# Joining the small steps of two slots in the RWKV time mixing

## The chip, the cores and the metric

The kernel runs on one NeuronCore of a Trainium2 chip. The metric is the device time of one execution in microseconds; lower is better. The program has no loops on the chip: Python writes out some 58,000 instructions, and a framework puts in the semaphores and orders the instructions of each engine when the program is built. TensorE (PE) multiplies matrices into PSUM, VectorE (DVE), ScalarE (ACT) and GpSimd (POOL) work elementwise, SyncE (SP) issues most DMAs.

## The reference

A trunk of two layers on 256 tokens of width 2048, batch 1, all float32. Layer 0 is RWKV-7 time mixing with 32 heads of 64, layer 1 attention in a band; each is followed by a squared-ReLU MLP. The change lies in the time mixing. There, with `r`, `k`, `v`, the decay `w` and the rates `a` and `g` projected from the normalised input:

```python
kk = heads(k * k_k)
kk = kk / jnp.maximum(jnp.sqrt(jnp.sum(kk * kk, axis=-1, keepdims=True)), 1e-12)
k = k * (1 + (a - 1) * k_a)
decay = jnp.exp(-jnp.exp(heads(w_log)))

def step(S, inp):
    r_t, w_t, k_t, v_t, kk_t, a_t = inp
    sa = jnp.einsum('bhvk,bhk->bhv', S, -kk_t)
    S = (S * w_t[:, :, None, :] + sa[..., None] * (kk_t * a_t)[:, :, None, :]
         + v_t[..., None] * k_t[:, :, None, :])
    y = jnp.einsum('bhvk,bhk->bhv', S, r_t)
    return S, y
```

The scan runs over the 256 tokens. Its output `y` is normalised by head, gets a bonus term `sum(r * k * r_k) * v`, is multiplied by `g` and projected by `w_o`.

## The kernel before

**Large products.** A projection weight comes from HBM in halves of 128x1024 float32 (`raw`, six buffers). `halves` (L371) turns each into two tiles: `wH` is a rounded copy made by ACT (L378), `wL` the rest, made by DVE (L381); each has three buffers (`W_BUFS`). `proj2` (L406) multiplies one k tile by two matmuls: `wH` with both parts of the activations (L412, 512 columns), `wL` with the first part (L413, 256 columns). A half weight holds eight k tiles.

**The chunked scan.** The 2048 channels are 16 pairs of heads (128 partitions each); a `Pair` object carries one pair through the time mixing in 36 steps. The 256 tokens are four chunks of 64. `early` (8 steps) makes the operands: decays (`cum`, `e0`, `e1`, `e2`), the normalised key `kk`, and `kr`, `bh`, `kh`, `vp`. `invert` (12 steps) forms for all chunks the products of `bh` with `kr` and inverts the unit triangular 64x64 matrices by levels: in each level, `tiles` (L107) multiplies 32x32 blocks twice, first with the transposed inverse so far (`tt`), then, after ACT has copied that product to `xs` (L243, at the last level L248), with `xs`. `late` (16 steps) goes through the four chunks in turn, three steps each (`g`; `sa`; the output `py` and the state `zs`), then normalises and gates. `head_sums` (L115) sums over each head by one matmul with a block matrix of ones; `each` (L105) is eight 64-row matmuls.

**The slots.** `layer_a` (L634) issues the work by slots (loop at L889). A pair starts every `SLOTS` = 8 slots, so four or five pairs are under way at once, each in another phase. In every slot each live pair takes one step, those in `invert` first, then `late`, then `early`. Behind them come two large steps (four k tiles) of the `k` and `r` projections of a coming pair (`proj_steps`), or, in the last 36 slots, steps of the output projection (`out_steps`). In three slots of four `self.ada()` adds a step of the adaLN vector, a product that DVE accumulates (L454). PE is held to this order by hand: each step's matmuls are tied behind the last PE instruction of the one before:

```python
for _, _, pr in sorted(live, key=lambda x: x[:2]):
    with tc.issue_after(last):
        next(pr.gen)
    last = self.last_pe()
```

The other engines' instructions are ordered by the framework when the program is built, by its own estimate of when each is ready. PSUM is shared out in tags: `ms` (`psm`, two buffers), `pj` (two), `gr` and `iv` (one each), `lt` (two, a bank per pair in `late`).

Of the kernel before, what the change touches and what calls it, by code (L numbers as in the profile page):

```python
# [24 lines left out]
NPAIR = D // P  # L25
# [52 lines left out]
class Pair:  # L78
# [13 lines left out]
    def s(self, name="s", bufs=8):  # L92
        return self.b.pw.tile([P, T], F32, tag=name, bufs=bufs, name=name)
# [28 lines left out]
    def early(self):  # L122
        b, nc, j, k, r, v, s, ch = self.b, self.b.nc, self.j, self.k, self.r, self.v, self.s, self.ch
        pw, vec, cst, e01 = b.pw, b.vec, b.cst, self.e01
        lw = self.lw
        z = b.psm()
        nc.tensor.matmul(z[:, 0:T], lw[:, 0, :], self.tw, start=True, stop=True)
        nc.tensor.matmul(z[:, T:2 * T], lw[:, 1, :], self.ta, start=True, stop=True)
# [12 lines left out]
        yield  # L141
        pss = b.psm()[:, :T]
        self.head_sums(pss, sq)
        cum = s()
        nc.vector.tensor_tensor_scan(out=cum, data0=cst("reset"), data1=sw, initial=0.0, op0=ALU.mult, op1=ALU.add)
        e0, e1 = e01[:, :, 0:C], e01[:, :, 1:C + 1]
        nc.scalar.activation(e1, ch(cum), AF.Exp, scale=-1.0)
        e2 = s()
        nc.scalar.activation(e2, cum, AF.Exp)
        self.pc = pw.tile([P, 4, 1], F32, tag="pc", bufs=4, name="pc")  # L150
        nc.gpsimd.tensor_copy(self.pc, e01[:, :, C:C + 1])
        yield
        rs, ss, rr = s(), s(), s()
        nc.vector.tensor_scalar(out=ss, in0=pss, scalar1=1e-24, scalar2=None, op0=ALU.max)
        nc.scalar.activation(rs, ss, AF.Ln)
        nc.scalar.activation(rs, rs, AF.Exp, scale=-0.5)
        nc.scalar.activation(rr, rs, AF.Square)
        km = s()
        nc.gpsimd.tensor_scalar(out=km, in0=a, scalar1=-1.0, scalar2=vec("k_a", j), op0=ALU.add, op1=ALU.mult)
        self.bh, self.kh = s("bh", 2), s("kh", 2)  # L160
        nc.gpsimd.tensor_tensor(out=self.bh, in0=a, in1=e2, op=ALU.mult)
        yield
        nc.vector.scalar_tensor_tensor(out=rr, in0=rr, scalar=-0.5, in1=ss, op0=ALU.mult, op1=ALU.mult)
        nc.vector.scalar_tensor_tensor(out=rs, in0=rr, scalar=1.5, in1=rs, op0=ALU.add, op1=ALU.mult)
        kk = s()
        nc.vector.scalar_tensor_tensor(out=kk, in0=k, scalar=vec("k_k", j), in1=rs, op0=ALU.mult, op1=ALU.mult)
        nc.vector.scalar_tensor_tensor(out=km, in0=km, scalar=1.0, in1=k, op0=ALU.add, op1=ALU.mult)
        yield
        kr = self.kr = self.big("kr", 4)
        nc.vector.tensor_tensor(out=kr[:, :, 0:C], in0=ch(kk), in1=e0, op=ALU.mult)  # L170
        nc.vector.tensor_tensor(out=self.bh, in0=self.bh, in1=kk, op=ALU.mult)
        nc.vector.tensor_tensor(out=kr[:, :, C:P], in0=ch(r), in1=e1, op=ALU.mult)
        rkp = s()
        nc.vector.scalar_tensor_tensor(out=rkp, in0=r, scalar=vec("r_k", j), in1=km, op0=ALU.mult, op1=ALU.mult)
        nc.vector.tensor_tensor(out=self.kh, in0=km, in1=e2, op=ALU.mult)
        yield

        self.vp = pw.tile([P, 4, C], F32, tag="vp", bufs=4, name="vp")
        pt = b.psm().rearrange("p (a c k) -> p a c k", a=2, c=4)
        self.each(lambda c: pt[:, 0, c, :], lambda c: ch(v)[:, c, :], lambda c: cst("cen"))  # L180
        nc.scalar.copy(self.vp, pt[:, 0])
        yield
        pbn = b.psm()[:, :T]
        self.head_sums(pbn, rkp)
        nc.vector.tensor_tensor(out=v, in0=pbn, in1=v, op=ALU.mult)
        yield
# [5 lines left out]
    def invert(self):  # L192
# [8 lines left out]


        ui = cst("ui").unsqueeze(1).to_broadcast([P, 4, P])
        ts = []
        for src in (bh, kh):
            t = s()
            nc.gpsimd.tensor_tensor(out=ch(t), in0=ch(src), in1=self.pc.to_broadcast([P, 4, C]), op=ALU.mult)
            ts.append(t)
        pg = pp.tile([P, 4, P], F32, tag="gr", bufs=1, name="gr")
        self.each(lambda c: pg[:, c, :], lambda c: ch(bh)[:, c, :], lambda c: kr[:, c, :])  # L210
        ar = self.ar = s("ar", 3)
        nc.vector.tensor_tensor(out=ch(ar), in0=pg[:, :, C:P], in1=ui[:, :, C:P], op=ALU.mult)


        da, co, u = half("da", 2), half("co", 2), half("u", 2)
        for i, K in enumerate(QS):
            n = H * (i % 2)
            nc.scalar.copy(da[K], pg[K, :, n:n + H])
            if i % 2 == 0:
                nc.scalar.mul(co[K], pg[K, :, H:C], -1.0)  # L220
        nc.gpsimd.tensor_tensor(out=u, in0=da, in1=every("lev0"), op=ALU.mult)
        als = b.pw.tile([P, 4, 4, H], F32, tag="al", bufs=2, name="al")
        nc.gpsimd.tensor_tensor(out=als, in0=da.unsqueeze(1).to_broadcast([P, 4, 4, H]),
                                in1=cst("levs").rearrange("p (l k) -> p l k", l=4).unsqueeze(2).to_broadcast([P, 4, 4, H]),
                                op=ALU.mult)
        yield
        nc.vector.tensor_tensor(out=u, in0=u, in1=every("eye_h"), op=ALU.add)

        pt = b.psm().rearrange("p (a c k) -> p a c k", a=2, c=4)
        for i, t in enumerate(ts):  # L230
# [4 lines left out]
        uf = self.u = b.uf[self.j % 2]  # L235
        down, up = ((0, 1), (2, 3)), ((1, 0), (3, 2))
        for l in range(1, 6):
            tt_, xs = half("tt", 2), half("xs", 2)
            nc.vector.transpose(out=tt_.rearrange("p c t -> p (c t)"), in_=u.rearrange("p c t -> p (c t)"))
            pi = self.corner(l)  # L240
            if l < 5:
                self.tiles(pi, als[:, l - 1], tt_, [(i, i) for i in range(4)])
# [9 lines left out]
            if l < 5:  # L252
                self.tiles(pi, xs, u, [(i, i) for i in range(4)])
                nc.vector.tensor_tensor(out=u, in0=u, in1=pi, op=ALU.add)
            else:
                self.tiles(pi, xs, u, up)
                for K in QS[::2]:
                    nc.vector.tensor_copy(uf[K, :, H:C], pi[K])
# [7 lines left out]
    def late(self):  # L266
# [7 lines left out]
        for c in range(4):  # L274
# [22 lines left out]
            if c < 3:  # L297
# [8 lines left out]
                else:  # L306
                    nc.vector.scalar_tensor_tensor(out=zn, in0=zs, scalar=pc[:, c, :], in1=pch[:, 2, :],
                                                   op0=ALU.mult, op1=ALU.add)
                zs = zn
            yield  # L310

        sq = self.square(py)
        yield
        var = b.psm()[:, :T]
        self.head_sums(var, sq)
        yield
        rg = s("sl", 1)
        nc.scalar.activation(rg, var, AF.Ln, scale=1.0 / C, bias=b.col(C_GN))
        nc.scalar.activation(rg, rg, AF.Exp, scale=-0.5)
        nc.vector.scalar_tensor_tensor(out=rg, in0=py, scalar=b.vec("ln_w", j), in1=rg, op0=ALU.mult, op1=ALU.mult)  # L320
        yield
        pg = b.psm()[:, :T]
        for i in range(2):
            mm(pg, lg[:, i, :], self.tg[:, i, :], start=(i == 0), stop=(i == 1))  # L324
# [5 lines left out]
class Body:  # L330
# [303 lines left out]
    def layer_a(self, st, sp):  # L634
# [198 lines left out]
        with ExitStack() as s1:  # L833
# [55 lines left out]
            for slot in range(S * NPAIR + Pair.STEPS):  # L889
# [342 lines left out]
```

## Time and profile before

| | |
|---|---|
| time, median of 3 runs | 2665.69 us (2665.36 to 2669.86) |
| profiled execution, its own time | 2668.82 us |
| its span, first to last instruction | 2667.0 us |
| mean granted clock of TensorE | 0.992 |
| time mixing by slots | about 203 to 711 us of the span |
| PE, DVE, ACT busy in 490 to 560 us | 69.29, 62.84, 40.58 us of 70 |

The profile is one execution with all engines' instructions. "Busy" is the time in which an engine had an instruction under way; matmuls are pipelined and their ends are modelled, so for PE the starts are what can be trusted. In a timeline a row gives the start, the duration, the engine, the source line, the operation, output and inputs by tile name, shapes and the count of merged instructions; square brackets give idle time ahead of it and what ended it. A float32 product appears as two matmul records. L12 is line 12 of the kernel.

### The profile page before, as it was taken

What the parts mean: (1) busy time and instruction counts of PE and PEld (TensorE: products, weight loads), DVE (VectorE), ACT (ScalarE), POOL (GpSimd) and SP (SyncE); (2) the same over time, 40 slices, a digit from 0 to 9 for tenths busy, and PEclk for the clock granted to TensorE, in tenths of its full rate; (3) what the DMA queues carried; (4) which work ended last, traced back from release to release, by engine and by line L of the source; (5) the groups of instructions that cost most, each with busy time, mean ns of one, the idle gap of its engine ahead of it and who ended that gap; (6) DMA issues with size and microseconds to landing.
All of it is one profiled execution on the core that took longest, in us unless ns stands there. A gap on an engine that the chain in (4) does not pass through costs nothing.

```text
span 2667.0 us, 58173 instructions
## 1 busy us (share of the span) xinstructions
PE 2594.2 (97%) x23596; PEld 2229.2 (84%) x23596; DVE 2112.8 (79%) x3102; ACT 1345.2 (50%) x2435; POOL 208.7 (8%) x320
## 2 busy tenths in 40 slices
PE   7999999999999999999999999999999999999997
PEld 4787777887899888888888998877898888888886
DVE  6788888889789888888888898899887555555555
ACT  3346455555456445355365554565564463453554
POOL 0002223322110000000001100000100000000002
PEclk9999999999999999999999999999999999999998
DMA  9976556566778888889898679887766555555553
GB/s 349 312 244 211 185 179 207 180 214 199 246 236 312 309 317 327 319 324 332 318 329 293 238 242 331 318 274 256 265 218 235 190 189 184 188 189 186 186 189 119
DMA packets 207149, 662.62 MB, mean 248 GB/s; under 512 B 21408, under 2 KB 54560, under 8 KB 206880
## 3 DMA queue, kind: packets, MB, share of 16 engines
q1 hardware_dynamic: 204816, 656.36, 71.5%
q8 instruction: 185, 3.03, 0.5%
q10 hardware_dynamic: 2064, 2.54, 0.3%
q14 instruction: 84, 0.69, 0.1%
HBM read 656.72 MB, written 2.10 MB: 247 GB/s over the span
## 4 chain that ended last, share of the span: by engine, by line
PE 85%; DVE 5%; issue 4%; DMA 4%; ACT 2%; POOL 1%; DVEq 0%; SPq 0%; ACTq 0%; POOLq 0%
PE pj L412 45%; PE pj L413 23%; PE pj L402 2%; PE pj L401 2%; PE pj L403 2%; DMA raw<-w_ada 1%; DVE wL L381 1%; PE iv L111 1%; DVE acc L454 1%; PE gr L105 1%; ACT wH L378 1%; PE ms L115 1%; PE o L401 1%; PE ms L324 0%; PE ms L105 0%
## 5 line engine op out<-in xcount | busy, mean ns | idle before, releaser
L381 DVE TENSOR_TENSOR wL<-raw,wH 128x1024 fp32r<-128x1024 f32 x772 | 941.1, 1220 | 354.9 <-ACT wH L378 347.0
L378 ACT CAST wH<-raw 128x1024 fp32r<-128x1024 f32 x772 | 805.8, 1045 | 799.7 <-PE pj L412 650.0
L412 PE MATMUL pj<-aHL,wH 128*128 128x512 f32 x3328 | 1202.0, 403 | 1.9 <-DVE x L945 1.4
L413 PE MATMUL pj<-aHL,wL 128*128 128x256 f32 x3328 | 936.1, 281 | 0.4 <-DVE wL L381 0.4
L412 PEld LDWEIGHTS pj<-aHL,wH 128*128 128x128 f32 x3328 | 629.4, 189 | 154.4 <-issue 8.7
L412 PE MATMUL pj<-hHL,wH 128*128 128x512 f32 x2048 | 723.0, 398 | 0.0
L413 PEld LDWEIGHTS pj<-aHL,wL 128*128 128x128 f32 x3328 | 629.4, 189 | 3.1 <-issue 0.8
L413 PE MATMUL pj<-hHL,wL 128*128 128x256 f32 x2048 | 574.4, 281 | 0.0
L412 PEld LDWEIGHTS pj<-hHL,wH 128*128 128x128 f32 x2048 | 384.6, 188 | 94.4 <-DVE hHL L991 0.2
L413 PEld LDWEIGHTS pj<-hHL,wL 128*128 128x128 f32 x2048 | 386.8, 189 | 0.1
L454 DVE SCALAR_TENSOR_TENSOR acc<-rada,ct,acc 128x1024 f32<-128x1024 f32 x256 | 327.2, 1278 | 8.5 <-DMA rada<-w_ada 7.6
L518 POOL TENSOR_TENSOR ss<-ss,sq 128x256 f32<-128x256 f32 x56 | 52.6, 940 | 1590.8 <-ACT sq L517 1590.5
L1016 DVE SCALAR_TENSOR_TENSOR x<-pj,mod,x 128x256 f32<-128x256 f32 x256 | 123.4, 482 | 58.6 <-PE pj L413 54.9
L454 DVE SCALAR_TENSOR_TENSOR acc<-raw,ct,acc 128x1024 f32<-128x1024 f32 x104 | 136.2, 1309 | 15.3 <-DMA raw<-w_ada 14.9
L988 ACT ACTIVATE t<-t 128x256 f32<-128x256 f32 x112 | 46.8, 418 | 123.5 <-DVE t L960 123.5
L401 PE MATMUL pj<-aHL,wH 128*128 128x258 f32 x384 | 109.0, 284 | 0.0
L402 PE MATMUL pj<-aHL,wH 128*128 128x258 f32 x384 | 108.9, 284 | 0.0
L403 PE MATMUL pj<-aHL,wL 128*128 128x258 f32 x384 | 108.0, 281 | 0.0
L403 PEld LDWEIGHTS pj<-aHL,wL 128*128 128x128 f32 x384 | 73.2, 191 | 0.2
L402 PEld LDWEIGHTS pj<-aHL,wH 128*128 128x128 f32 x384 | 72.6, 189 | 0.1
L401 PEld LDWEIGHTS pj<-aHL,wH 128*128 128x128 f32 x384 | 72.2, 188 | 0.2
L990 ACT ACTIVATE t<-t 128x256 f32<-128x256 f32 x128 | 53.4, 417 | 3.4
(249 smaller groups left out, 2815.5 us busy)
## 6 DMA issues: line engine op xcount, KB each, us to landing
raw<-w_up SPq DMA_DIRECT2D x256, 512.0 KB, 4.2
raw<-w_down SPq DMA_DIRECT2D x256, 512.0 KB, 4.3
rada<-w_ada SPq DMA_DIRECT2D x209, 512.0 KB, 5.8
raw<-w_ada SPq DMA_DIRECT2D x111, 512.0 KB, 4.3
rada<-w_ada_kv SPq DMA_DIRECT2D x64, 512.0 KB, 6.1
rawa<-w_ada SPq DMA_DIRECT2D x32, 512.0 KB, 6.9
rawa<-w_ada_t SPq DMA_DIRECT2D x32, 512.0 KB, 7.5
raw<-w_k SPq DMA_DIRECT2D x32, 512.0 KB, 4.0
```

What stands on the lines that cost most here:

```text
L378: nc.scalar.copy(Hf, raw)
L381: eng.tensor_tensor(out=Lf, in0=raw, in1=Hf, op=ALU.subtract)
L401: nc.tensor.matmul(ps, H[:, i, :], a(kt)[:, 0, :], start=(first and kt == 0), stop=False)
L402: nc.tensor.matmul(ps, H[:, i, :], a(kt)[:, 1, :], start=False, stop=False)
L403: ins = nc.tensor.matmul(ps, L[:, i, :], a(kt)[:, 0, :], start=False, stop=(last and kt == KT - 1))
L412: nc.tensor.matmul(ps, H[:, i, :], a(kt), start=(kt == 0), stop=False)
L413: ins = nc.tensor.matmul(ps[:, 0, :], L[:, i, :], a(kt)[:, 0, :], start=False, stop=(kt == KT - 1))
L454: nc.vector.scalar_tensor_tensor(out=self.acc, in0=raw, scalar=ck, in1=self.acc, op0=ALU.mult, op1=ALU.add)
L518: (eng or nc.gpsimd).tensor_tensor(out=self.ss, in0=self.ss, in1=sq, op=ALU.add)
L988: nc.scalar.activation(t, t, AF.Relu)
L990: nc.scalar.activation(t, t, AF.Square)
L1016: nc.vector.scalar_tensor_tensor(out=x, in0=ps[:, i, :], scalar=self.mods[(layer, 5)][:, n:n + 1], in1=x, op0=ALU.mult, op1=ALU.add)
```

## The change

The loop issues large steps in odd slots alone, twice as many: the small steps of an even slot and of the odd slot after it then stand together on PE, and eight k tiles (a half weight) follow. `self.ada()` stays in the slots where it was.

Within a pair, work moves between steps, counted from the pair's first slot:
- the head sum for the key norm goes from step 2 to step 4, what is made of it one step later; `vp` goes from step 6 to step 4, and `kr`, `bh` from step 5 to step 6;
- `bh` and `kh` times the chunk's decay (`ts`) are made on GpSimd at the end of `early` (step 6), not at the head of `invert`;
- in `invert`, `u` is transposed (`turned`) right after it is made, not at the head of the step that reads it; the addition of the unit matrix goes from DVE to GpSimd; `ar` is made a step later; the two copies into `uf` at the last level go from DVE to ACT;
- in `late`, the square of `py` is taken with the last chunk, the variance goes into the pair's own `lt` bank, and the exponential and the `ln_b` term shift by a step.

Instructions are otherwise the same in number and shape.

```diff
@@ early
         yield
-        pss = b.psm()[:, :T]
-        self.head_sums(pss, sq)
         cum = s()
...
         nc.gpsimd.tensor_copy(self.pc, e01[:, :, C:C + 1])
         yield
+        km = s()
+        nc.gpsimd.tensor_scalar(out=km, in0=a, scalar1=-1.0, scalar2=vec("k_a", j), op0=ALU.add, op1=ALU.mult)
+        self.bh, self.kh = s("bh", 2), s("kh", 2)
+        nc.gpsimd.tensor_tensor(out=self.bh, in0=a, in1=e2, op=ALU.mult)
+        yield
+        pss = b.psm()[:, :T]
+        self.head_sums(pss, sq)
         rs, ss, rr = s(), s(), s()
         nc.vector.tensor_scalar(out=ss, in0=pss, scalar1=1e-24, scalar2=None, op0=ALU.max)
...
-        km = s()
-        nc.gpsimd.tensor_scalar(out=km, in0=a, scalar1=-1.0, scalar2=vec("k_a", j), op0=ALU.add, op1=ALU.mult)
-        self.bh, self.kh = s("bh", 2), s("kh", 2)
-        nc.gpsimd.tensor_tensor(out=self.bh, in0=a, in1=e2, op=ALU.mult)
-        yield
+        self.vp = pw.tile([P, 4, C], F32, tag="vp", bufs=4, name="vp")
+        pt = b.psm().rearrange("p (a c k) -> p a c k", a=2, c=4)
+        self.each(lambda c: pt[:, 0, c, :], lambda c: ch(v)[:, c, :], lambda c: cst("cen"))
+        nc.scalar.copy(self.vp, pt[:, 0])
+        nc.vector.scalar_tensor_tensor(out=km, in0=km, scalar=1.0, in1=k, op0=ALU.add, op1=ALU.mult)
+        rkp = s()
+        nc.vector.scalar_tensor_tensor(out=rkp, in0=r, scalar=vec("r_k", j), in1=km, op0=ALU.mult, op1=ALU.mult)
+        yield
+        kr = self.kr = self.big("kr", 4)
...
-        nc.vector.scalar_tensor_tensor(out=km, in0=km, scalar=1.0, in1=k, op0=ALU.add, op1=ALU.mult)
-        yield
-        kr = self.kr = self.big("kr", 4)
+        nc.vector.tensor_tensor(out=self.kh, in0=km, in1=e2, op=ALU.mult)
+        yield
+        nc.vector.tensor_tensor(out=self.bh, in0=self.bh, in1=kk, op=ALU.mult)
         nc.vector.tensor_tensor(out=kr[:, :, 0:C], in0=ch(kk), in1=e0, op=ALU.mult)
-        nc.vector.tensor_tensor(out=self.bh, in0=self.bh, in1=kk, op=ALU.mult)
         nc.vector.tensor_tensor(out=kr[:, :, C:P], in0=ch(r), in1=e1, op=ALU.mult)
-        rkp = s()
-        nc.vector.scalar_tensor_tensor(out=rkp, in0=r, scalar=vec("r_k", j), in1=km, op0=ALU.mult, op1=ALU.mult)
-        nc.vector.tensor_tensor(out=self.kh, in0=km, in1=e2, op=ALU.mult)
-        yield
-
-        self.vp = pw.tile([P, 4, C], F32, tag="vp", bufs=4, name="vp")
-        pt = b.psm().rearrange("p (a c k) -> p a c k", a=2, c=4)
-        self.each(lambda c: pt[:, 0, c, :], lambda c: ch(v)[:, c, :], lambda c: cst("cen"))
-        nc.scalar.copy(self.vp, pt[:, 0])
+        self.ts = []
+        for src in (self.kh, self.bh):
+            t = s()
+            nc.gpsimd.tensor_tensor(out=ch(t), in0=ch(src), in1=self.pc.to_broadcast([P, 4, C]), op=ALU.mult)
+            self.ts.insert(0, t)
         yield
@@ invert
-        ts = []
-        for src in (bh, kh):
-            t = s()
-            nc.gpsimd.tensor_tensor(out=ch(t), in0=ch(src), in1=self.pc.to_broadcast([P, 4, C]), op=ALU.mult)
-            ts.append(t)
...
-        ar = self.ar = s("ar", 3)
-        nc.vector.tensor_tensor(out=ch(ar), in0=pg[:, :, C:P], in1=ui[:, :, C:P], op=ALU.mult)
...
+        def turned():
+            t = half("tt", 2)
+            nc.vector.transpose(out=t.rearrange("p c t -> p (c t)"), in_=u.rearrange("p c t -> p (c t)"))
+            return t
...
         nc.gpsimd.tensor_tensor(out=u, in0=da, in1=every("lev0"), op=ALU.mult)
+        nc.gpsimd.tensor_tensor(out=u, in0=u, in1=every("eye_h"), op=ALU.add)
+        tn = turned()
...
         yield
-        nc.vector.tensor_tensor(out=u, in0=u, in1=every("eye_h"), op=ALU.add)
+        ar = self.ar = s("ar", 3)
+        nc.vector.tensor_tensor(out=ch(ar), in0=pg[:, :, C:P], in1=ui[:, :, C:P], op=ALU.mult)
...
-            tt_, xs = half("tt", 2), half("xs", 2)
-            nc.vector.transpose(out=tt_.rearrange("p c t -> p (c t)"), in_=u.rearrange("p c t -> p (c t)"))
+            tt_, xs = tn, half("xs", 2)
...
                 nc.vector.tensor_tensor(out=u, in0=u, in1=pi, op=ALU.add)
+                tn = turned()
...
-                    nc.vector.tensor_copy(uf[K, :, H:C], pi[K])
+                    nc.scalar.copy(uf[K, :, H:C], pi[K])
@@ late
                 zs = zn
+            if c == 3:
+                sq = self.square(py)
             yield
 
-        sq = self.square(py)
-        yield
-        var = b.psm()[:, :T]
+        yield
+        var = bank[:, 0, :]
         self.head_sums(var, sq)
-        yield
         rg = s("sl", 1)
         nc.scalar.activation(rg, var, AF.Ln, scale=1.0 / C, bias=b.col(C_GN))
+        yield
         nc.scalar.activation(rg, rg, AF.Exp, scale=-0.5)
         nc.vector.scalar_tensor_tensor(out=rg, in0=py, scalar=b.vec("ln_w", j), in1=rg, op0=ALU.mult, op1=ALU.mult)
+        nc.vector.scalar_tensor_tensor(out=rg, in0=v, scalar=b.vec("ln_b", j), in1=rg, op0=ALU.add, op1=ALU.add)
         yield
...
-        nc.vector.scalar_tensor_tensor(out=rg, in0=v, scalar=b.vec("ln_b", j), in1=rg, op0=ALU.add, op1=ALU.add)
@@ layer_a
-                if slot < S * NPAIR:
-                    if slot % S == 0:
-                        dense = proj_steps(pairs[slot // S])
-                    todo = 16 // S
-                else:
-                    if outs is None:
-                        self.y_hl = self.new_hl()
-                        outs = dense = out_steps()
-                    todo = OUTS * (slot + 1 - S * NPAIR) // Pair.STEPS - n_out
-                    n_out += todo
-                with tc.issue_after(last):
-                    for _ in range(todo):
-                        next(dense, None)
+                if slot % 2:
+                    if slot < S * NPAIR:
+                        if slot % S == 1:
+                            dense = proj_steps(pairs[slot // S])
+                        todo = 32 // S
+                    else:
+                        if outs is None:
+                            self.y_hl = self.new_hl()
+                            outs = dense = out_steps()
+                        todo = OUTS * (slot + 1 - S * NPAIR) // Pair.STEPS - n_out
+                        n_out += todo
+                    with tc.issue_after(last):
+                        for _ in range(todo):
+                            next(dense, None)
```

More of the change, by code (lines that the diff above doesn't have):

```diff
@@ L166, in early @@
         nc.vector.scalar_tensor_tensor(out=kk, in0=k, scalar=vec("k_k", j), in1=rs, op0=ALU.mult, op1=ALU.mult)
-        nc.vector.scalar_tensor_tensor(out=km, in0=km, scalar=1.0, in1=k, op0=ALU.add, op1=ALU.mult)
-        yield
-        kr = self.kr = self.big("kr", 4)
-        nc.vector.tensor_tensor(out=kr[:, :, 0:C], in0=ch(kk), in1=e0, op=ALU.mult)
-        nc.vector.tensor_tensor(out=self.bh, in0=self.bh, in1=kk, op=ALU.mult)
-        nc.vector.tensor_tensor(out=kr[:, :, C:P], in0=ch(r), in1=e1, op=ALU.mult)
-        rkp = s()
-        nc.vector.scalar_tensor_tensor(out=rkp, in0=r, scalar=vec("r_k", j), in1=km, op0=ALU.mult, op1=ALU.mult)
         nc.vector.tensor_tensor(out=self.kh, in0=km, in1=e2, op=ALU.mult)
         yield
-        self.vp = pw.tile([P, 4, C], F32, tag="vp", bufs=4, name="vp")
-        pt = b.psm().rearrange("p (a c k) -> p a c k", a=2, c=4)
-        self.each(lambda c: pt[:, 0, c, :], lambda c: ch(v)[:, c, :], lambda c: cst("cen"))
-        nc.scalar.copy(self.vp, pt[:, 0])
+        nc.vector.tensor_tensor(out=self.bh, in0=self.bh, in1=kk, op=ALU.mult)
+        nc.vector.tensor_tensor(out=kr[:, :, 0:C], in0=ch(kk), in1=e0, op=ALU.mult)
+        nc.vector.tensor_tensor(out=kr[:, :, C:P], in0=ch(r), in1=e1, op=ALU.mult)
+        self.ts = []
[3 more added lines that the diff above has]
+            self.ts.insert(0, t)
         yield
@@ L226, in invert @@
         yield
-        nc.vector.tensor_tensor(out=u, in0=u, in1=every("eye_h"), op=ALU.add)
+        ar = self.ar = s("ar", 3)
+        nc.vector.tensor_tensor(out=ch(ar), in0=pg[:, :, C:P], in1=ui[:, :, C:P], op=ALU.mult)
         pt = b.psm().rearrange("p (a c k) -> p a c k", a=2, c=4)
-        for i, t in enumerate(ts):
+        for i, t in enumerate(self.ts):
             self.each(lambda c: pt[:, i, c, :], lambda c: ch(t)[:, c, :], lambda c: cst("eye"))
```

## The prediction

> **What bounds the kernel now.** I read the page first, for the engines and the chain that ended last, then the table of stages, to see whether the time mixing is held by the same engine.
>
> ```profile
> span 2667.0 us, 58173 instructions
> PE 2594.2 (97%) x23596; PEld 2229.2 (84%) x23596; DVE 2112.8 (79%) x3102; ACT 1345.2 (50%) x2435; POOL 208.7 (8%) x320
> PE 85%; DVE 5%; issue 4%; DMA 4%; ACT 2%; POOL 1%; DVEq 0%; SPq 0%; ACTq 0%; POOLq 0%
> ```
>
> ```profile
> 203.00:290.00 87.00, 77.05 (x1028) 63.67 (x1029) 74.80 (x129) 46.26 (x111) 20.58 (x25) 0.94 0.64 206
> 290.00:627.00 337.00, 330.60 (x6950) 271.08 (x6949) 291.11 (x557) 183.76 (x521) 94.97 (x132) 1.00 0.59 189
> 627.00:711.00 84.00, 79.21 (x1592) 68.20 (x1591) 71.28 (x120) 35.63 (x102) 13.72 (x21) 1.00 0.70 232
> ```
>
> The second fence is the table of stages (stretch, length, then busy time of PE, PEld, DVE, ACT, POOL). The change touches these 508 us alone: the pairs filling up, the steady middle, the tail with the output projection. In the middle PE is busy 98%, DVE 86%, ACT 55%. PE sets the time, so an edit is worth what it does to the sequence of PE instructions and to PE's waits. What other engines gain or lose counts only through those waits.
>
> **What joining two slots saves.** The timeline of PE (start, duration) shows one block of large products and the small ones on both sides.
>
> ```profile
> 480.49 0.28 PE L302 MATMUL lt<-vp,bk 64*64 64x64 f32 x4
> 480.61 0.63 PE L105 MATMUL ms<-csts,v 64*64 64x64 f32 x16
> 481.17 0.50 PE L412 MATMUL pj<-aHL,wH 128*128 128x512 f32 x1
> 481.63 0.40 PE L412 MATMUL pj<-aHL,wH 128*128 128x512 f32 x1
> 481.98 0.40 PE L412 MATMUL pj<-aHL,wH 128*128 128x512 f32 x1
> 482.78 0.45 PE L111 MATMUL iv<-u,xs 32*32 32x32 f32 x32
> ```
>
> The block runs from 481.17 to 482.78, 1.61 us for four k tiles of two matmuls each. In its middle a k tile takes 481.98 - 481.63 = 0.35 us, so four cost 1.42 us (0.355 by the finer starts) and 0.19 us is the price of entering and leaving. Joined blocks of eight k tiles pay it once: 0.19 us saved for each two slots, 0.76 us for the eight slots of one pair. The exit of the first small group, which went into a large product, now goes from a 64- or 128-wide product into a 32-wide one. No row shows this step. The nearest, 64-wide into 128-wide (included in the 0.56 us from 480.61 to 481.17) and 128-wide into 32-wide (included in the block), both cost; I take the same as for the exit it replaces, that is nothing gained and nothing lost, with 0.1 us per join either way as bounds. [...]
>
> **What moving the head sum costs.** The 128-wide sum for the key norm (L143) stood last in its slot; it goes two slots later, ahead of the 64-wide products of vp (L180).
>
> ```profile
> 463.65 0.70 PE L115 MATMUL ms<-sq,csts 128*128 128x256 f32 x2
> 464.28 0.33 PE L291 MATMUL lt<-mk,vp 64*64 64x64 f32 x4
> ```
>
> ```profile
> 466.63 0.34 PE L111 MATMUL ms<-tt,co 32*32 32x32 f32 x10
> 467.27 0.33 PE L280 MATMUL lt<-vp,mk 64*64 64x64 f32 x4
> 467.65 0.70 PE L115 MATMUL ms<-sq,csts 128*128 128x256 f32 x2
> 468.00 0.58 PE L412 MATMUL pj<-aHL,wH 128*128 128x512 f32 x1
> ```
>
> In the old place it takes 468.00 - 467.65 = 0.35 us; a sum with 64-wide products behind it takes 464.28 - 463.65 = 0.63 us. That is +0.28 us per pair. The vp products and all others keep their count. The large steps take their DMAs along: the weight halves (L393) and lw (L856) are issued on SP's queue up to one slot later, the lora half lg (L277) where it was. A half is cast four slots or more before its products and lw is read only when the next pair begins, so one slot of 3.5 us is covered and I cost this at nothing; were it not, a cast (1.04 us) and wL (1.23 us) would show ahead of a large block.
>
> **Waits that go.** In the list of waits of the steady middle (11 pairs) PE waits for a PSUM buffer that L154 still reads.
>
> ```profile
> PEld ms L324 <- DVE s L154: 2.1, 6, 0.4
> PE ms L324 <- DVE s L154: 1.2, 4, 0.3
> ```
>
> The sum and its reader L154 leave that slot, and the variance (L314) leaves this pool, so the wait goes: (2.1 + 1.2) / 11 = 0.30 us per pair. Two copies of L258 go from DVE to ACT, and the add of L227 from DVE to GpSimd. DVE loses 18.6 + 9.0 us in the whole stage; none of it is on PE's path, since the users come two slots later. The price of the moved add on GpSimd lies between the 282 ns of L254, the same shape on DVE, and the 1161 ns of L227; I take 0.7 us, and the levels (als) and the transpose are needed only two slots on, behind a block of 3 us.
>
> ```profile
> L227 DVE TENSOR_TENSOR u<-u,csts 128x128 f32<-128x128 f32 x16 | 18.6, 1161 | 6.3 <-POOL u L221 5.3
> L254 DVE TENSOR_TENSOR u<-u,iv 128x128 f32<-128x128 f32 x64 | 18.1, 282 | 9.0 <-PE iv L111 8.0
> L258 DVE COPY uf<-ms 32x128 f32<-32x128 f32 x32 | 9.0, 281 | 0.9 <-PE ms L111 0.6
> ```
>
> The three sums so far: -0.76 + 0.28 - 0.30 = -0.78 us per pair.
>
> **Waits that come.** Most operands are now made a slot or more ahead. One kind is not: inside a level of the inversion the even step's product goes through an ACT copy (xs) to the odd step's product, and these two steps now stand in one small group with no large block between. Here are ACT, DVE and PE where a small group begins.
>
> ```profile
> 467.34 1.03 ACT L378 CAST wH<-raw 128x1024 fp32r<-128x1024 f32 x1
> 468.39 0.52 ACT L248 COPY xs<-ms 32x128 f32<-32x128 f32 x2
> 468.94 0.27 ACT L243 COPY xs<-iv 128x128 f32<-128x128 f32 x1
> ```
>
> ```profile
> 479.58 1.04 ACT L378 CAST wH<-raw 128x1024 fp32r<-128x1024 f32 x1 [1.24 <-PE pj L412]
> 480.54 0.26 ACT L243 COPY xs<-iv 128x128 f32<-128x128 f32 x1
> ```
>
> ```profile
> 480.66 1.23 DVE L381 TENSOR_TENSOR wL<-raw,wH 128x1024 fp32r<-128x1024 f32 x1 [0.28 <-ACT wH L378]
> 481.80 0.22 DVE L305 COPY zs<-lt 128x64 f32<-128x64 f32 x1
> ```
>
> ```profile
> 479.59 0.45 PE L111 MATMUL iv<-tt,al 32*32 32x32 f32 x32
> 483.16 0.33 PE L291 MATMUL lt<-mk,vp 64*64 64x64 f32 x4
> 483.68 0.28 PE L283 MATMUL lt<-zs,kr 64*64 64x64 f32 x4
> ```
>
> Each half weight that PE finishes frees a buffer; ACT then casts the next half at once (1.04 us, released by pj L412). A half is eight k tiles, exactly a joined block, so every joined block ends with such a cast, and xs stands behind it on ACT; DVE's wL (1.23 us) follows and zs stands behind that. With the slots numbered from the start of a pair:
> - Slots 2 and 3. The even group (two inversions, L280, L283) lasts 467.65 - 466.63 = 1.02 us. The last 32-row copy ends at 468.39 + 0.52 = 468.91, 1.57 us after the cast began. PE waits 0.55 us.
> - Slots 6 and 7. The even group without vp lasts 480.61 - 479.59 = 1.02 us; xs is done at 480.80, 1.22 us in: 0.20 us. Then come the inversion (0.38 us, 482.78 to 483.16) and L291 to L280 (483.16 to 483.68, 0.52 us), so zs is due at 1.22 + 0.90 = 2.12 us; it is there at 482.02, 2.44 us in: 0.32 us.
> - Slots 0, 1 and 4, 5 have more products between, and the copy is done 459.40 + 0.27 - 458.20 = 1.47 us in (rows below). In the first the even group lasts past the start of L128, 460.25 - 458.20 = 2.05 us; in the other the inversion (0.38), the head sum (0.63) and vp (0.56) alone last 1.57 us, and two late steps come on top. No wait.
>
> ```profile
> 458.20 0.45 PE L111 MATMUL iv<-tt,al 32*32 32x32 f32 x32
> 460.25 0.59 PE L128 MATMUL ms<-ta,lw 96*128 96x256 f32 x2
> ```
>
> ```profile
> 459.40 0.27 ACT L243 COPY xs<-iv 128x128 f32<-128x128 f32 x1
> ```
>
>
> I add 0.05 us of handing over for three waits: 0.55 + 0.20 + 0.32 + 0.15 = +1.22 us per pair. Bounds: nothing, if the copies come first on ACT (a 32-wide product's 0.45 us and the copy's 0.27 us end 0.7 us in, inside the 1.02 us), and 2.5 us, if one more accumulation of 1.28 us (row below) precedes zs.
>
> ```profile
> 481.94 1.27 DVE L454 SCALAR_TENSOR_TENSOR acc<-raw,ct,acc 128x1024 f32<-128x1024 f32 x1
> 459.72 0.70 PE L127 MATMUL ms<-tw,lw 96*128 96x256 f32 x2
> 487.44 0.70 PE L127 MATMUL ms<-tw,lw 96*128 96x256 f32 x2
> ```
>
> **The sum.** One pair lasts 487.44 - 459.72 = 27.7 us, so the middle's 337 us hold 12 pairs: 12 x (1.22 - 0.78) = +5.3 us. The filling and the tail have 28 more joins (-0.19 x 28 = -5.3 us) and some 5 pairs' worth of waits, fewer products lying between (5 x 1.22 = +6.1 us): +0.8 us. Together +6.1 us on the profiled execution's 2668.82 us (span 2667.0 and 1.8 around it), that is 2674.9 us. That execution lies 3.1 us above the median of the runs, 2665.69; on the median I get 2671.8 us, 0.23% slower.
>
> **Rivals.**
> 1. *The copies come in time.* If ACT takes xs ahead of the cast, no wait comes. Then -0.78 x 12 - 5.3 = -14.7 us: 2651 us; with half of the waits 2661 us. For it: ACT is idle 45% of the middle, and the order on ACT is fixed at build time, not by who is ready first on the chip. Against it: the cast of the half weight stands ahead of xs in both rows above, and its release lies at the same point in the new order.
> 2. *DVE falls behind.* Two accumulations stand between the even and odd small steps where large products stood. If one of them (1.28 us) precedes zs in each eight slots, that is 1.28 x 12 = 15 us more: 2687 us on the median. It decides from the point where zs comes later than 2.1 us after the block's end. For it: DVE is 86% busy. Against it: it loses 28 us of work in the change.
> [...]
>
> **Chances.** The forecast (waits as above, 2662 to 2682 us) 0.48; rival 1 0.34; rival 2 0.12; rival 3 0.06. About 0.2% (5.3 us) is what a measurement of this kernel can tell from no change, so "same" is 2660.4 to 2671.0 us. Of the forecast's 0.48 I put 0.19 there and 0.29 above, since the bounds of the waits reach further up than down. Rival 1 gives 0.32 to faster and 0.02 to the same, rival 2 all to slower, rival 3 0.04 to the same and 0.01 to each side. Faster 0.33, same 0.25, slower 0.42. Both signs are open: the forecast's own range is 2662 to 2682 us, the full one 2650 to 2688 us, from rival 1 to rival 2.
>
> **What would show it.** In the changed trace a block of eight k tiles lasts 3.0 us, with half as many blocks. The sum of small groups grows by the waits: in slots 2, 3 and 6, 7 the second L111 group should start 1.6 and 1.25 us after the cast did, and PE should list waits for ACT xs L243 or L248 and DVE zs. L324 should wait no more. The forecast is wrong if the xs copies start within 0.6 us of the block's end, if a pair lasts under 27 us or over 29.5 us, or if large blocks wait for weights.

## The result and the profile after

The changed kernel takes 2687.40 us (median of 4 runs, 2685.64 to 2690.02), the kernel before, run beside it, 2666.48 us. The ratio is 1.0076 (95% interval 1.0061 to 1.009): slower by 0.76%, or 21 us. The prediction had 2671.8 us, 6.1 us slower. One run of the kernel that only joins, below, took 6351 us beside four of 2691 to 2707 us and is left out of its figures.

The page of the changed kernel shows the same picture as before, only longer: PE busy 97%, and 86% of the chain that ended last.

```profile
span 2688.2 us, 58164 instructions
PE 2604.1 (97%) x23596; PEld 2237.7 (83%) x23596; DVE 2091.0 (78%) x3054; ACT 1352.7 (50%) x2467; POOL 211.0 (8%) x336
PE 86%; DVE 5%; ACT 3%; issue 3%; DMA 2%; POOL 1%; DVEq 0%; SPq 0%; ACTq 0%; POOLq 0%
```

DVE lost 21.8 us of work, and it did not help. The table of stages (stretch, length, then busy time and instructions of PE, PEld, DVE, ACT, POOL, the granted clock, DMA share, GB/s), in the first two of the prediction's three stretches, is read with care, since the work of the stages has shifted:

```profile
203.00:290.00 87.00, 80.27 (x1173) 66.36 (x1172) 75.11 (x133) 52.09 (x127) 24.26 (x37) 0.96 0.66 214
290.00:627.00 337.00, 315.20 (x6338) 256.78 (x6330) 252.81 (x468) 169.81 (x489) 87.68 (x126) 0.96 0.55 178
```

The filling now does 1173 matmuls in 87 us where it did 1028. The middle does 6338 in 337 us where it did 6950, PE idles 21.8 of them where it idled 6.4, and the granted clock is 0.96 instead of 1.00. For equal work the stretch has to be cut where pair 3 and pair 14 start their first lora product. So cut, the same 11 pairs (6399 and 6394 matmuls) stand first in the kernel before, then in the changed one:

```profile
288.00:601.00 313.00, 306.60 (x6399) 251.42 (x6396) 268.76 (x507) 167.66 (x474) 88.21 (x121) 1.00 0.60 193
```

```profile
283.00:623.00 340.00, 318.20 (x6394) 259.55 (x6392) 254.93 (x474) 171.98 (x494) 90.11 (x132) 0.96 0.55 176
```

The middle is 27 us longer: PE is idle 340.0 - 318.2 = 21.8 us instead of 6.4 (+15.4), and the same matmuls keep it busy 11.6 us longer, at a lower clock. By the starts of those products the filling is 5.2 us shorter, the middle 27.5 us longer and the tail (to the last pair's L324, now L331) 1.2 us shorter: +21.1 us, and the spans differ by 21.2.

**Waits on ACT and DVE, as forecast.** Undisturbed groups show them. First PE in slots 2 and 3 (start, duration), from the end of one large block to the end of the next, then ACT beside it:

```profile
446.13 0.34 PE L111 MATMUL ms<-tt,co 32*32 32x32 f32 x10
447.50 0.72 PE L111 MATMUL ms<-u,xs 32*32 32x32 f32 x16 [0.28 <-ACT xs L252]
448.16 0.45 PE L111 MATMUL iv<-u,xs 32*32 32x32 f32 x32
449.87 0.50 PE L418 MATMUL pj<-aHL,wH 128*128 128x512 f32 x1
452.86 0.45 PE L111 MATMUL iv<-tt,al 32*32 32x32 f32 x32
```

```profile
446.12 1.04 ACT L384 CAST wH<-raw 128x1024 fp32r<-128x1024 f32 x1 [0.69 <-PE pj L418]
447.19 0.54 ACT L252 COPY xs<-ms 32x128 f32<-32x128 f32 x2
447.75 0.27 ACT L247 COPY xs<-iv 128x128 f32<-128x128 f32 x1
```

The cast starts as the large block ends, the two copies wait behind it, and PE's second products wait for each of the copies in turn (0.28 us ahead of 447.50, and again inside the 0.66 us to 448.16). The group lasts 449.87 - 446.13 = 3.74 us, the large block 452.86 - 449.87 = 2.99 us. In slots 6 and 7 PE waits for xs and then for zs:

```profile
431.43 0.45 PE L111 MATMUL iv<-tt,al 32*32 32x32 f32 x32
432.68 0.45 PE L111 MATMUL iv<-u,xs 32*32 32x32 f32 x32
433.91 0.33 PE L285 MATMUL lt<-vp,mk 64*64 64x64 f32 x4 [0.28 <-DVE zs L310]
434.64 0.58 PE L418 MATMUL pj<-aHL,wH 128*128 128x512 f32 x1
```

```profile
431.42 1.04 ACT L384 CAST wH<-raw 128x1024 fp32r<-128x1024 f32 x1 [2.34 <-PE pj L418]
432.37 0.26 ACT L247 COPY xs<-iv 128x128 f32<-128x128 f32 x1
```

**Waits that were not forecast.** In four of the eleven pairs the group of slots 2 and 3 takes 6 to 7.6 us instead of 3.74. Here is one that begins at 412.65, on PE, ACT, DVE and POOL, with the table of two stretches:

```profile
413.43 0.28 PE L288 MATMUL lt<-zs,kr 64*64 64x64 f32 x4
416.58 0.86 PE L111 MATMUL ms<-u,xs 32*32 32x32 f32 x15 [2.87 <-ACT xs L252]
```

```profile
411.40 0.81 ACT L134 ACTIVATE s<-s 128x256 f32<-128x256 f32 x2 [3.07 <-DVE s L132]
414.59 0.42 ACT L145 ACTIVATE e<-s 128x256 f32<-128x256 f32 x1 [0.21 <-DVE s L143]
414.92 0.40 ACT L147 ACTIVATE s<-s 128x256 f32<-128x256 f32 x1
415.22 1.03 ACT L384 CAST wH<-raw 128x1024 fp32r<-128x1024 f32 x1
416.27 0.54 ACT L252 COPY xs<-ms 32x128 f32<-32x128 f32 x2
```

```profile
405.71 1.28 DVE L460 SCALAR_TENSOR_TENSOR acc<-raw,ct,acc 128x1024 f32<-128x1024 f32 x1 [3.24 <-DMA raw<-w_ada]
408.60 1.78 DVE L460 SCALAR_TENSOR_TENSOR acc<-raw,ct,acc 128x1024 f32<-128x1024 f32 x1
410.69 0.31 DVE L216 STREAM_TRANSPOSE tt<-u 128x128 f32<-128x128 f32 x1 [0.31 <-POOL u L225]
410.93 0.84 DVE L132 TENSOR_SCALAR s<-ms,vecs 128x256 f32<-128x256 f32 x2
```

```profile
407.23 2.08 POOL L228 TENSOR_TENSOR al<-da,csts 128x512 f32<-128x512 f32 x1
409.26 1.40 POOL L225 TENSOR_TENSOR u<-u,csts 128x128 f32<-128x128 f32 x1
```

```profile
413.00:417.00 4.00, 1.13 (x52) 0.85 (x37) 3.79 (x7) 3.72 (x10) 3.34 (x5) 0.83 0.69 230
417.00:423.00 6.00, 6.00 (x64) 4.62 (x63) 4.66 (x7) 0.96 (x5) 1.46 (x1) 0.55 0.52 168
```

Read it upwards from PE. The products at 416.58 wait for xs. On ACT xs stands behind the cast, and the cast here stands behind the two exponentials of the next pair's decay (L145, L147), which end a chain that DVE starts with L132. L132 came late because DVE stood behind an accumulation that waited 3.24 us for its w_ada and behind the early transpose (L216), which waited for GpSimd's add of the unit matrix (L225). The kernel asks for that add ahead of `al`, but GpSimd's order has it behind `al` in every pair. The timelines of all eleven pairs agree, counted from a group's first inversion product (L111): where an accumulation and the transpose stand between the lora product and L132, L132 starts 1.7 to 2.3 us ahead of the group and xs 3.0 to 3.6 us into it (four pairs); where they don't, L132 starts 4.9 to 6.4 us ahead and xs at 1.1 us or earlier (seven). PE had nothing for 2.87 us, and the granted clock fell: 1.00 up to 415.5, 0.55 from 417 to 423. PE's and DVE's lists of waits in the middle total this up (us, times, longest):

```profile
PE ms L111 <- ACT xs L252: 11.3, 10, 2.9
PE lt L285 <- DVE zs L310: 6.8, 10, 2.5
```

```profile
DVE acc L460 <- DMA raw<-w_ada: 16.7, 15, 3.2
DVE tt L216 <- POOL u L225: 12.7, 11, 1.7
```

### The profile page after: what moved, and what is told of

It reads as the page before. It is cut to its first block, busy times and chain, and to the rows that moved or that the text cites. A ratio compares the mean times of both kernels' runs of the same rounds, so it can differ in the third digit from the quotient of the medians.

```text
span 2688.2 us, 58164 instructions
## 1 busy us (share of the span) xinstructions
PE 2604.1 (97%) x23596; PEld 2237.7 (83%) x23596; DVE 2091.0 (78%) x3054; ACT 1352.7 (50%) x2467; POOL 211.0 (8%) x336
## 4 chain that ended last, share of the span: by engine, by line
PE 86%; DVE 5%; ACT 3%; issue 3%; DMA 2%; POOL 1%; DVEq 0%; SPq 0%; ACTq 0%; POOLq 0%
PE pj L418 45%; PE pj L419 23%; PE pj L408 2%; PE pj L407 2%; PE pj L409 2%; ACT wH L384 1%; PE iv L111 1%; DVE wL L387 1%; PE gr L105 1%; DVE acc L460 1%; PE ms L115 1%; PE ms L331 1%; PE ms L105 1%; PE o L407 0%; PE t L775 0%
```

## The experiments

Two theories stood against each other. A: the large blocks release a cast at the same point at which xs is wanted, and ACT's order (cast first, in some pairs exponentials first) makes PE wait. B: the steps moved between engines and slots cost the time by themselves, the adaLN accumulation (rival 2) or the early transposes on DVE above all. Each experiment ran beside its own runs of the kernel before (medians of 2668.25 to 2668.84 us, where the first comparison had 2666.48), so across experiments the ratios compare better than the medians.

**Each half alone.** The moved steps with the old loop, and the new loop with the old steps.

```diff
 moves_only: the changed Pair, in layer_a
-                if slot % 2:
...
-                        todo = 32 // S
+                    todo = 16 // S
 join_only: the Pair of before, in layer_a the reverse
```

> The moved steps of a pair with the old loop (two large steps in every slot). Theory A, the loss comes from the joined groups, in which a copy of ACT and a state of DVE are due within one group: then the moves alone cost nothing, the wait of L324 goes (0.3 us a pair) and the moved head sum costs 0.2 us: 2660 to 2668 us. Rival B, the moved operands themselves delay DVE (the early transpose waits for GpSimd's added unit matrix): most of the 21 us is here, 2678 to 2688 us.

> The old steps of a pair with the new loop (large steps in odd slots alone, twice as many). Theory A: the old steps read what was made in the same step or the one before, so more waits fall into the joined groups than in the changed kernel: 2695 to 2725 us. Rival B, the moves make the loss: 2660 to 2670 us, 0.19 us saved at each join.

Measured: moves alone 2678.44 us, ratio 1.0036 (1.0023 to 1.005); joining alone 2701.21 us, 1.012 (1.01 to 1.0139). Both halves lose (10 and 33 us), and together they lose less than the sum, so the moves repair part of what joining breaks. That the moves cost 10 us without any joined block was a miss for theory A. PE's waits in the middle of that kernel name the transposes: 8.9 us in 11 times (7.3 us of it ahead of `iv`), where the kernel before has 2.1 us in 4. The first line is the list's, then the longest wait on PE, and DVE ahead of it:

```profile
PE iv L111 <- DVE tt L216: 7.3, 8, 2.3
```

```profile
397.05 0.45 PE L111 MATMUL iv<-tt,al 32*32 32x32 f32 x32 [2.26 <-DVE tt L216]
```

```profile
394.20 1.29 DVE L460 SCALAR_TENSOR_TENSOR acc<-raw,ct,acc 128x1024 f32<-128x1024 f32 x1 [3.58 <-DMA raw<-w_ada]
395.80 0.28 DVE L258 TENSOR_TENSOR u<-u,iv 128x128 f32<-128x128 f32 x1
396.60 0.30 DVE L216 STREAM_TRANSPOSE tt<-u 128x128 f32<-128x128 f32 x1
```

L216 is a helper's line and stands for five transposes of each pair. The early one, which waits for GpSimd's add, is none of these 11: each of them is a later level's transpose, behind the add of L258. In five an accumulation stands between the two, in the other six shortly ahead of the add. So here PE waits for transposes that DVE takes late, and what makes them late was not tried by itself.

In the kernel that only joins, PE waits for xs (6.8 us) and for lora sums that DVE has not yet read out (6.5 us in 4 times).

**The cast behind the copies; the first transpose later.** In the first, the second half weight of each projection is cast only once the xs copies of its slots are issued on ACT. It is also asked for one large block later than before, and its rest `wL` on DVE follows the cast, so the run does not part the cast from `wL`. In the second, the first transpose is asked for one step later, still one step ahead of its reader.

```diff
 cast_behind
-                    self.wnext = None if src is None else self.weight(src)
+                    raws = [] if src is None else [self.raw(src[:, i * HK * P:(i + 1) * HK * P]) for i in range(KT // HK)]
+                    self.wnext = [self.halves(r_) for r_ in raws[:1]]
...
+                        if kt == HK and raws:
+                            with tc.issue_after(self.last_xs.ins) if self.last_xs else nullcontext():
+                                self.wnext.append(self.halves(raws[1]))
 late_turn
-        tn = turned()
         yield
+        tn = turned()
```

> The changed kernel, with the second half weight of each projection cast only behind the xs copies of the even slot (slots 2 and 6 of a pair). Theory A: xs is done some 0.8 us (slot 6) and 1.1 us (slot 2) into the group instead of 1.25 and 1.6, and zs is no longer behind wL: 1.2 to 1.5 us a pair less, 14 to 18 us over 12 pairs: 2668 to 2674 us, and the groups of slots 2, 3 and 6, 7 last 2.9 and 2.6 us instead of 3.7 and 3.2. Rival, the long groups come from a late DVE or GpSimd: 2680 to 2688 us.

> The changed kernel, with the first transpose of an inversion one step later (step 9, not 8), so that DVE does not wait for GpSimd ahead of the decay's operands. If the few groups of 6 to 7.6 us in slots 2, 3 come from that wait (tt waits for GpSimd's u, 12.7 us in 11 times), they fall to 3.7 us, and the half clock behind them goes: 10 to 16 us less, 2671 to 2678 us. If they come from the weights of the adaLN vector (acc waits for its DMA), nothing changes: 2683 to 2690 us.

Measured: 2676.11 us, 1.0031 (1.0019 to 1.0042), and 2680.12 us, 1.0041 (1.0027 to 1.0054). Each takes back a part, 11 and 7 us by the medians (12 and 9 by the ratios), with intervals apart from that of the changed kernel (1.0061 to 1.009), and neither reaches the kernel before. With the cast behind, the group of slots 6 and 7 falls to 2.6 us in six of eleven pairs, but that of slots 2 and 3 still lasts 4.2 to 6.5 us in eight: in these the early transpose stands ahead of L132, and xs comes late. With the later transpose DVE waits 3.3 us for L225 in the middle instead of 12.7, and three pairs instead of four have xs 2.6 us or more into the group; in these an accumulation still stands ahead of L132. The 2680.12 us lie between the two expectations. So both theories hold a part: one early transpose for each pair costs some 7 us here, though it had seemed free.

**The exponentials behind the copies.** In the long groups L145 and L147 come late and stand ahead of the cast and xs. They were tied behind the last xs copy, alone, with the cast, and with cast and transpose.

```diff
 exp_behind; with the edits above: cast_exp (cast), three_behind (cast and transpose)
+        with b.tc.issue_after(b.last_xs.ins) if b.last_xs else nullcontext():
+            nc.scalar.activation(e1, ch(cum), AF.Exp, scale=-1.0)
+            nc.scalar.activation(e2, cum, AF.Exp)
```

> The changed kernel with the decay's two exponentials alone put behind the xs copies; the cast stays ahead of them. Theory A, each of the two orders on ACT has its own share: the joined group of slots 2, 3 keeps its shortest length of 3.74 us (the cast), and the long ones of 6 us and more, where the exponentials wait for DVE ahead of xs, go; its mean falls from 5.0 to about 4.0 us and the half clock with it: 2668 to 2676 us. Rival, the cast is the whole of it: 2684 to 2689 us.

> The three orders without the later transpose (cast and exponentials behind the xs copies). If the transpose's place matters beside them: 2663 to 2670 us, with longer waits of DVE for GpSimd's u. If the two orders on ACT are enough: 2656 to 2661 us, within 3 us of the three together.

> The changed kernel with three orders at once: the second half weight is cast behind the xs copies, the decay's two exponentials (steps 2) go behind them too, and the first transpose comes a step later. Theory A, what is left of the loss is the chain on ACT ahead of xs in slots 2, 3 (in the run with the cast behind, that group still lasted 3.8 to 6.5 us in most pairs, 3.2 us in the best): the group falls to 3.2 to 3.8 us throughout, a pair to 27.5 to 28.3 us, and with the 8 us that the filling gained the time is 2655 to 2666 us. Rival, DVE itself is late (accumulations that wait for their DMA): the group stays over 4 us and the time between 2668 and 2678 us.

| kernel | median us | ratio to before (95%) |
|---|---|---|
| changed kernel | 2687.40 | 1.0076 (1.0061 to 1.009) |
| exponentials behind | 2683.72 | 1.0061 (1.0048 to 1.0075) |
| cast behind | 2676.11 | 1.0031 (1.0019 to 1.0042) |
| cast and exponentials | 2664.74 | 0.9987 (0.9979 to 0.9996) |
| cast, exponentials, transpose | 2658.55 | 0.9955 (0.9942 to 0.9969) |

The exponentials alone do much less than expected, and their interval overlaps that of the changed kernel: the cast is still in the way. Together the two bring 22.7 us, more than 3.7 + 11.3 us apart; in ratios the surplus is 0.0029, with an uncertainty of some 0.0025 from the four intervals. The three edits turn 0.76% slower into 0.45% faster, which beats the kernel before. In that kernel the middle (11 pairs), PE in slots 2 and 3, and ACT beside it:

```profile
283.00:593.00 310.00, 304.38 (x6388) 251.48 (x6387) 255.35 (x474) 168.78 (x492) 79.91 (x132) 1.00 0.61 195
```

```profile
430.26 0.34 PE L111 MATMUL ms<-tt,co 32*32 32x32 f32 x10
431.07 0.28 PE L289 MATMUL lt<-zs,kr 64*64 64x64 f32 x4
431.28 0.49 PE L111 MATMUL ms<-u,xs 32*32 32x32 f32 x16
433.43 0.50 PE L419 MATMUL pj<-aHL,wH 128*128 128x512 f32 x1
```

```profile
430.75 0.54 ACT L253 COPY xs<-ms 32x128 f32<-32x128 f32 x2 [1.28 <-PE ms L111]
431.48 0.42 ACT L147 ACTIVATE e<-s 128x256 f32<-128x256 f32 x1
432.74 1.05 ACT L385 CAST wH<-raw 128x1024 fp32r<-128x1024 f32 x1
```

Now xs comes first, then the exponentials, then the cast. From the second pair of the middle on, xs starts 0.5 us behind the group's first inversion product in all ten. In half of them an accumulation still stands ahead of L132, but without the early transpose L132 is hardly late (4.3 us or more ahead). The even group runs into the odd one without idle time, and the whole group lasts 433.43 - 430.26 = 3.17 us instead of 3.74. Against the changed kernel the middle is 30 us shorter: PE idles 5.6 us instead of 21.8 (-16.2), and the same work keeps it busy 13.8 us less, at a clock of 1.00 instead of 0.96. Waits and the low clock that follows the long ones thus share the loss about half and half (the ends of matmuls are modelled, so this split is rough). The low clock goes away only with both ties: from 283 to 610 us it is 0.97 with the cast or the exponentials alone behind xs, 1.00 with both.

**The adaLN accumulations elsewhere.** Two steps behind slots 3, 5 and 7 of each eight instead of one in three slots of four; in the changed kernel, and in the kernel with the three edits (there also with the old pattern in the tail).

```diff
 ada_357, three_ada (three_ada_mid: in the pairs' slots alone)
-                if slot >= 2 * S and slot % 4 < 3:
-                    self.ada()
+                if slot >= 2 * S and slot % S in (3, 5, 7):
+                    self.ada(2)
```

> The changed kernel with only the adaLN steps moved (two each behind slots 3, 5 and 7). Rival 2 of the prediction, accumulations between the even and odd small steps delay zs and the decay's chain: 6 to 15 us less, 2672 to 2681 us, and the groups of 6 us and more go. Theory A, the order on ACT alone: 2684 to 2690 us.

> As the run with three orders, and the adaLN steps go two at a time behind the odd slots 3, 5 and 7, none in slots 0 to 2, so that no accumulation that waits for its DMA stands ahead of the decay's chain. If those accumulations make the long groups: 2 to 8 us less than with the three orders alone. If not: within 3 us of it, or more, where two accumulations in a row (2.6 us) now delay the transposes or zs in slots 4 to 7.

> The three orders with the adaLN steps behind slots 3, 5 and 7 up to the tail, and in the old slots in the tail, where the other version lost 3.6 us (112.2 against 108.6 us): 2651 to 2655 us. If the tail's loss only followed from vectors that were not yet finished: 2655 to 2658 us.

Measured: 2704.18 us, 1.0128 (1.0114 to 1.0142), outside both expectations; with the three edits 2656.36 us, 0.9958 (0.9945 to 0.9971), and 2657.82 us, 0.9963 (0.9948 to 0.9977), neither to be told from 0.9955. The same edit costs 17 us in one kernel (14 by the ratios) and nothing in the other. The timeline of DVE in the first, ahead of a group that begins at 347.53 and has xs at 350.58, shows why:

```profile
342.63 2.06 DVE L460 SCALAR_TENSOR_TENSOR acc<-raw,ct,acc 128x1024 f32<-128x1024 f32 x1 [0.86 <-DMA raw<-w_ada]
345.00 0.31 DVE L216 STREAM_TRANSPOSE tt<-u 128x128 f32<-128x128 f32 x1 [0.31 <-POOL u L225]
345.23 0.83 DVE L132 TENSOR_SCALAR s<-ms,vecs 128x256 f32<-128x256 f32 x2
```

Accumulation and transpose now stand ahead of L132 in six pairs instead of four, and in these xs starts 2.5 to 3.1 us into the group. In the second kernel no L132 is late (4.4 to 5.7 us ahead in every pair), so the place of the accumulations doesn't matter there. What a late L132 does once xs is tied ahead is seen in the kernel with cast and exponentials alone: in seven of its eleven pairs L132 starts only 2.3 to 2.9 us ahead, yet xs comes 0.6 to 1.2 us into the group, which lasts 3.3 to 3.8 us. The rest of that delay comes from the other steps of the decay on ACT (L134 to L140), which still stand ahead of xs. That PE's waits pass from L132 over ACT to xs is so shown from both sides: by tying xs ahead, and by making L132 late more often.

**Joining where pairs are few.** Since the filling had become shorter, the kernel before was joined in its first 32 slots alone.

```diff
 join_ramp: the layer_a of before
+                joined = slot < 4 * S
+                if slot % 2 or not joined:
...
+                        todo = 32 // S if joined else 16 // S
```

> The kernel before with the slots joined only in the first 32, in which the pairs fill up and large blocks wait for weights; old steps of a pair throughout. In the changed kernel this stretch took 68.7 us against 73.9, with the joined loop alone 68.0. If that gain belongs to the filling itself: 4 to 6 us faster than before, 2661 to 2664 us. If it is only work put off into the next slots: no change, 2665 to 2669 us.

Measured: 2665.6 us, 0.999 (0.9981 to 0.9999), some 3 us where 5 had been taken from the filling of the changed kernel, and hardly to be told from no change.

## Why the prediction was right or wrong

**Right: what bounds the kernel, the sign and the place.** PE sets the time, the joined blocks last 2.99 us as said (3.0), the L324 wait is gone, and PE waits for ACT xs and DVE zs where the prediction put them: the second inversion product starts 1.38 us (said: 1.6) and 1.26 us (1.25) after the cast.

**Right: the size of these waits in undisturbed groups.** Slots 2 and 3 last 3.74 us, without the waits 3.17: 0.57 us (forecast 0.55). Slots 6 and 7 last 434.64 - 431.43 = 3.21 us; with the three edits such a group without a wait runs from 416.18 to 418.78, 2.60 us:

```profile
416.18 0.45 PE L111 MATMUL iv<-tt,al 32*32 32x32 f32 x32
418.78 0.59 PE L419 MATMUL pj<-aHL,wH 128*128 128x512 f32 x1
```

That is 0.61 us (forecast 0.20 + 0.32). Together 1.18 us against 1.22 with the handing over. The 0.05 us taken for the latter was an estimate; in this group the copy xs ends at 432.37 + 0.26 = 432.63 and PE starts at 432.68, 0.05 us later. Rival 1, that xs would come first, fell in the changed kernel; the three edits show that it is what happens when ACT's order is tied.

**Too high: the savings.** Put together from undisturbed groups and blocks in turn, a pair of the changed kernel would last 5.40 + 3.00 + 3.74 + 3.00 + 4.22 + 2.99 + 3.21 + 3.09 = 28.65 us against 27.7. No pair of the middle but the first, which is shorter in its first slots, comes that low; the next lasts 29.3 us. Less the 1.18 us of waits that is 27.5: 0.2 us saved, where joins and head sum had 0.76 - 0.28 = 0.48. The join itself is worth 0.22 us (two old blocks of 1.61 less one of 2.99 to 3.00), more than the 0.19; slots 0 and 1, at 5.40 us, give back 0.3 us. That the new exit, into a 32-wide product, costs as much as the old one was the author's assumption; no run shows that step by itself. For 11 pairs this accounts for 11 x 0.95 = 10.5 of the 27.5 us.

**Wrong: "the levels (als) and the transpose are needed only two slots on", the moved add and its users costed at nothing.** They were costed by when their products are read. What stands behind the transpose in the queue of DVE was not asked. The add itself was sized well (the page gives 600 ns where 0.7 us was taken). But it starts late, behind `al` on GpSimd, and the early transpose waits for it 12.7 us in 11 times; L132 stands behind the transpose, and from L132 a chain leads over ACT's exponentials to the cast and xs. Making the first transpose one step later takes 7 us off the changed kernel. The moves without any joined block cost 10 us, mostly by another way: PE's waits for the later levels' transposes grow from 2.1 to 8.9 us; which of the moves makes these late stays open, since no run isolated it.

**Wrong: the upper bound of the waits.** It had one accumulation of 1.28 us ahead of zs, 2.5 us in all for a pair. The groups of slots 2 and 3 reach 7.6 us, and the low clock behind them was no term at all: the large block that follows one takes up to 4.18 us instead of 3.0. The four pairs with such groups last 32.2 to 34.1 us, together 16.9 us over the 28.65; the other seven lie 7.9 us over it together, about as much as the eleven of the kernel before lie over 27.72 (7.6 us). So about 17 of the 27.5 us belong to the four. By the prediction's own sign, a pair over 29.5 us, the forecast is wrong: the eleven last 30.9 us on average, eight of them over 29.5. The time lies outside the forecast's 2662 to 2682 us, at the far end of the full range, at rival 2's 2687 us, and that it meets this number is mostly luck. Rival 2 had a part of the mechanism, an accumulation that holds DVE, but in another place: it was to stand ahead of zs between the even and the odd steps, and in the four pairs it stands ahead of L132, a block earlier, and reaches PE over ACT and xs. In its own place it shows once, in the pair that starts at 374: accumulations at 395.24 and 396.78 stand ahead of `wL` and zs (399.50), PE waits 2.51 us for zs, and slots 6 and 7 last 5.44 us instead of 3.21.

**Too low: the gain in the filling and the tail.** They got 6.4 us shorter, where +0.8 was forecast. The waits costed there (6.1 us) came: PE's lists give 5.7 us for xs and zs in the filling and 2.4 us in the tail. What the sum left out is what went: in the filling of the kernel before, PE waited 8.3 us for transposes (L239) and 1.6 us for an operand of the bonus sum (L174), and neither wait is left. PE's idle time there falls from 9.9 to 6.6 us for the same 958 matmuls, and its busy time by 1.8 us.

## What to carry to other kernels

Moving an operand earlier is free for the one who reads it, not for what it now stands ahead of: of every moved instruction ask what it waits for, and what is behind it on its engine. A large block that ends releases work on other engines (here a 1 us cast) exactly when the small steps behind it need a 0.27 us copy; if the order on that engine is left to a planner, tie the big one behind the small one. Where several obstacles stand in the same queue, removing one alone can show less than its share, so judge them together. When a list of waits names a helper's line, look up which of its calls it was before blaming one.

## What the runs showed of the hardware

**A short wait cost twice.** Within the 2.87 us without a matmul (413.71 to 416.58) the granted clock fell from 1.00 (up to 415.5) to 0.50 (from 416), it was 0.55 from 417 to 423, and eight k tiles took up to 4.18 us behind such waits where an undisturbed block takes 2.99. The length of the wait alone does not settle it: behind waits of 2.19 to 2.87 us in the four long groups the mean clock of the next 6 us was 0.50 to 0.72, behind that of 2.51 us at 399.77 it stayed 1.00, with a block of 3.09 us. What decides stays open here.

**DVE and GpSimd were slow side by side.** The al at 407.23 took 2.08 us where the group's mean is 1.23, the accumulation beside and behind it 1.78 us where its neighbour took 1.28, the add behind that 1.40 us where the mean is 0.60:

```profile
L225 POOL TENSOR_TENSOR u<-u,csts 128x128 f32<-128x128 f32 x16 | 9.6, 600 | 0.0
L228 POOL TENSOR_TENSOR al<-da,csts 128x512 f32<-128x512 f32 x16 | 19.6, 1226 | 0.0
```

The three long instructions lie side by side in time, on GpSimd from 407.23 to 410.66 and on DVE from 408.60 to 410.38; whether the one engine slowed the other was not shown, since no run here tested it by itself.
